# Ten Strassen pairs that accumulate two partial sums in PSUM banks, and a last product in two column halves

## The chip, the cores and the metric

The kernel runs on one core of a Trainium2 chip. The metric is the device time of one execution in microseconds (us). Lower is better. The engines are named as in the profile: PE is TensorE (PEld its weight loads), DVE is VectorE, ACT is ScalarE, POOL is GpSimd and SP is SyncE, which only issues DMAs here. PSUM is the memory into which PE accumulates, in banks of 128x512 fp32; SBUF is the on-chip memory for everything else.

## What the kernel must compute

One block of a hybrid encoder, in fp32, for 1024 positions of width 1024 (cut to what matters):

```python
h = rmsnorm(x, norm_g)
proj = h @ w_in                       # split into q, k, v, za, u, vs, zs, gm
q, k = partial_rope(q), partial_rope(k)
a = window_sink_attention(q, k, v, att_sinks)            # 16 heads, 2 kv heads, window 128
a = (a * silu(za)) @ w_att_out
sgo = chunked_spatial_gating(gelu(u), gelu(vs), sg_w, sg_b, sg_ln_g, sg_ln_b)
sgo = (sgo * silu(zs)) @ w_sg_out
ga, gs = split(sigmoid(gm + b_merge))                    # one merge gate per branch
y = ga * a + gs * sgo
out = rmsnorm(x + y @ w_o, final_g)
```

## The kernel before

**Products.** fp32 accuracy is reached by splitting every operand into a high part in fp32r and a low part that holds the rest (`split`: ACT copies the high part, DVE subtracts it). `product` (L340) multiplies four 128-row blocks of the contraction, three terms each (high x high, high x low, low x high), so it is 12 matmuls of 128x512 into one bank.

**Pairs.** The large products run in the Strassen-Winograd form: `gemm_pair` (L358) handles two 128-row blocks of output as a 2x2 block product with seven products instead of eight. The weights' parts 0 to 6 (w11, w12, the sums s1 to s4 and w22, made on DVE or by DMAs) stand in tiles `wh` and `wl`; the activations' seven forms b11, t1, t2, b21, t3, b22 and t4 stand in the tiles `T_...h` and `T_...l`. The order in a pair is this. b11 goes into the accumulator `acc` (a bank of the pool mm), which ACT copies to x11 (L368). t1 goes into a bank of the pool o, named t5; ACT writes its negative to x22 (L372). t2 accumulates on acc, and ACT copies that to x12 (L375). b21 goes into a fresh bank (pool tp or o), and DVE adds it to x11 (L380): output block (0, 0). t3 accumulates on acc; DVE subtracts acc from x22 (L385): block (1, 1). b22 accumulates on t5; DVE adds it to x12 (L389): block (0, 1). t4 accumulates on acc: block (1, 0). x11, x12, x22 and the tile for block (1, 0) are `xtile()`s, a ring of five SBUF tiles of 128x512. Each is given to the caller's `finish`, which works on it in place and stores it to DRAM; a tile can be taken again when its store has landed.

**Stages.** In order of time: RMSNorm and the forms of its result; the pairs of u, vs and k and v; of q; of z and of the merge gates with attention between their products (`softmax_stage` L1271, whose pieces run as hooks of the pairs); four pairs of za; four s pairs (the spatial branch's output product); four a pairs (attention's output product); the first products of the four token pairs (L1821 to L1825); the token pairs p = 0 to 3 with w_o, the residual, and the last RMSNorm. `finish` of za is Silu on ACT, later a multiply on DVE (`finish_silu`, L1558 and L1559) and a store to a_dr through POOL's queue (`put`, L466). That of an s pair is a Sigmoid gate on ACT (L1684), a multiply on DVE (L1691 or L1693) and a store to y_dr through POOL's queue. That of an a pair is the same with a DMA on POOL's queue that adds onto y_dr; for the last a pair DVE adds what is there (L1788) and SP stores it. The forms t1 to t4 of the next stage are read back from these stores and made between the products: sums by DMAs that add (`bq<-bq`, L202 on POOL's queue), high parts on ACT (L154, L159) and low parts on DVE (L155, L160).

**What sets the order.** The program is written in one order by hand; each engine executes its own instructions strictly in that order, waiting at each for semaphores. `hook` and `split_next` put pieces of other work between the products. `after` adds an order without a wait, and `paced` lets a DMA wait for the last result named in `pace`.

**Attention.** In a step of `softmax_stage` PE makes the scores of two halves c = 0, 1 into banks of the pool sc (L1295), DVE finds the largest by two operations per half (L1303 and L1304, the bound), and ACT takes four exponentials with it (L1308), which release the banks. `split_q` (L1087) splits rotated queries into high parts (ACT, L1092) and low parts (DVE, L1094) and stores both through SP.

**The end.** For the last token pair, p = 3, the order of the products is b22, t3, b21, t4. `add_and_square` (L1846) adds a product to the residual on DVE (L1849) and sums squares on ACT (L1851); `rstd_of` (L132) makes the reciprocal root with a Sqrt on ACT and five small operations on DVE, the last two at L146 and L147; `scale_and_store` (L1861) multiplies by the root and by the gain `g_out`, on ACT (L1868) or DVE (L1871), and stores.

## Time and profile before

| | |
|---|---|
| three runs shown | 1278.79, 904.73 and 905.77 us; median 905.77 |
| the profiled execution, its own time | 905.2 us |
| its span, first to last instruction | 903.4 us |
| around the span | 1.8 us |
| granted clock of PE | 0.998 |
| PE, DVE, ACT and POOL busy | 890.3, 691.3, 529.3 and 149.5 us |
| pairs of za | from 588 to 664 us |
| s pairs, then a pairs | 664 to 741, 742 to 819 us |
| first products of the token pairs, then the token pairs | 819.5 to 830.4, 830.4 to 896 us |

Times in the profile count from the first instruction. A row of the timeline gives the start in us, the duration in us, the engine, the line, the operation, output<-inputs, shapes, and in brackets how long the engine stood idle just before and what released it. Names of tiles stand without their numbers. PE's matmuls follow each other every 0.227 us while a row shows some 0.39 us for one, since they are pipelined and their ends are modelled. A group's row gives after the bar its busy time in us, the mean in ns of one instruction, and the idle time before them with its releasers. In the chain of waits a row names what the end was waiting for at that time.

### The profile page before, as it was taken

The page shows a single profiled execution, that of the slowest core. Times are in us where ns is not written, and L with a number is a line of the kernel's source. Part 1 is how long each engine was busy: PE and PEld are TensorE (multiplying, and loading weights), DVE is VectorE, ACT ScalarE, POOL GpSimd, SP SyncE. Part 2 cuts the span into 40 slices and gives each one's busy share as a digit, 9 for nine tenths or more (in the row PEclk, how much of TensorE's full clock was granted, in tenths as well). Part 3 has the DMA queues.
Part 4 walks back from the last instruction along what each step waited for, and adds up shares of the span by engine and source line. Part 5 has one row for each costly group of instructions (what it writes and reads, how often), then busy time and mean ns, then how long its engine had stood idle before and what let it go on. Part 6 is the DMA issues. An engine that isn't in the chain of part 4 may idle for free.

```text
span 903.4 us, 13232 instructions
## 1 busy us (share of the span) xinstructions
PE 890.3 (99%) x4292; PEld 742.7 (82%) x4292; DVE 691.3 (77%) x1259; ACT 529.3 (59%) x1061; POOL 149.5 (17%) x213
## 2 busy tenths in 40 slices
PE   8999999999999999999999999999999999999996
PEld 6788888888888888888888888888877887888885
DVE  7879966666686788887878888747797488579996
ACT  7865533334445567667677676654675375467443
POOL 2322222203030001111110111101121121110012
PEclk9999999999999999999999999999999999999999
DMA  9998888958778768888687789899899788998632
GB/s 328 212 246 227 264 204 176 171 152 266 255 251 284 216 181 215 209 168 207 177 230 224 232 247 234 209 332 352 301 291 339 287 230 241 301 301 263 208 120 113
DMA packets 132750, 213.77 MB, mean 237 GB/s; under 512 B 12777, under 2 KB 61161, under 8 KB 132682
## 3 DMA queue, kind: packets, MB, share of 16 engines
q1 hardware_dynamic: 110072, 149.74, 50.0%
q0 software_dynamic: 22464, 62.93, 31.3%
q8 instruction: 34, 0.56, 0.3%
q14 instruction: 34, 0.28, 0.1%
q10 hardware_dynamic: 146, 0.27, 0.1%
HBM read 147.74 MB, written 86.11 MB: 259 GB/s over the span
## 4 chain that ended last, share of the span: by engine, by line
PE 82%; DMA 8%; issue 7%; ACT 1%; POOL 1%; DVE 1%; SPq 0%; POOLq 0%; ACTq 0%; DVEq 0%
PE ps_mm L350 34%; PE ps_o L350 26%; PE ps_sc L1295 3%; PE ps_tp L708 2%; PE ps_sc L350 2%; PE ps_mm L708 2%; PE ps_o L1380 2%; PE ps_o L708 2%; PE ps_tp L1339 2%; DMA bq<-bq 2%; PE ps_tp L970 2%; PE ps_tp L350 2%; DMA a_dr<-x 1%; PE ps_sc L708 1%; DMA y_dr<-x 1%
## 5 line engine op out<-in xcount | busy, mean ns | idle before, releaser
L159 ACT CAST wh<-s 128x1024 fp32r<-128x1024 f32 (+1 forms) x79 | 79.2, 1005 | 89.3 <-PE ps_mm L350 42.7
L160 DVE TENSOR_TENSOR wl<-wr,wh 128x512 fp32r<-128x512 f32 (+1 forms) x77 | 72.1, 937 | 51.3 <-ACT wh L159 50.4
L160 DVE TENSOR_TENSOR wl<-s,wh 128x1024 fp32r<-128x1024 f32 (+1 forms) x79 | 92.6, 1173 | 11.6 <-ACT wh L159 11.5
L159 ACT CAST wh<-wr 128x512 fp32r<-128x512 f32 (+1 forms) x77 | 63.1, 820 | 59.9 <-PE ps_mm L350 33.4
L350 PE MATMUL ps_o<-T_t1h,wh 128*128 128x512 f32 x148 | 58.6, 396 | 0.0
L350 PE MATMUL ps_o<-T_b22h,wh 128*128 128x512 f32 x148 | 58.3, 394 | 0.0
L350 PE MATMUL ps_o<-T_t1h,wl 128*128 128x512 f32 x148 | 57.8, 391 | 0.0
L350 PE MATMUL ps_o<-T_b22l,wh 128*128 128x512 f32 x148 | 57.8, 391 | 0.0
L350 PE MATMUL ps_o<-T_b22h,wl 128*128 128x512 f32 x148 | 57.7, 390 | 0.0
L350 PE MATMUL ps_o<-T_t1l,wh 128*128 128x512 f32 x148 | 57.6, 389 | 0.0
L350 PE MATMUL ps_mm<-T_t3h,wh 128*128 128x512 f32 x140 | 55.1, 394 | 1.5 <-ACT x L375 1.5
L1308 ACT ACTIVATE pr<-ps_sc,sm 128x192 f32<-128x192 f32 (+2 forms) x128 | 50.8, 409 | 8.8 <-DVE sm L1304 6.3
L350 PE MATMUL ps_mm<-T_t4h,wh 128*128 128x512 f32 x140 | 55.1, 394 | 0.2 <-DVE x L385 0.2
L350 PE MATMUL ps_mm<-T_b11h,wh 128*128 128x512 f32 x140 | 54.9, 392 | 0.0
L350 PE MATMUL ps_mm<-T_b11h,wl 128*128 128x512 f32 x140 | 54.7, 391 | 0.0
L350 PE MATMUL ps_mm<-T_t4h,wl 128*128 128x512 f32 x140 | 54.7, 391 | 0.0
L350 PE MATMUL ps_mm<-T_b11l,wh 128*128 128x512 f32 x140 | 54.7, 391 | 0.0
L350 PE MATMUL ps_mm<-T_t3h,wl 128*128 128x512 f32 x140 | 54.7, 391 | 0.0
L350 PE MATMUL ps_mm<-T_t2h,wl 128*128 128x512 f32 x140 | 54.6, 390 | 0.0
L350 PE MATMUL ps_mm<-T_t2h,wh 128*128 128x512 f32 x140 | 54.6, 390 | 0.0
L350 PE MATMUL ps_mm<-T_t2l,wh 128*128 128x512 f32 x140 | 54.5, 390 | 0.0
L350 PE MATMUL ps_mm<-T_t4l,wh 128*128 128x512 f32 x140 | 54.5, 389 | 0.0
(400 smaller groups left out, 2396.7 us busy)
## 6 DMA issues: line engine op xcount, KB each, us to landing
wr<-in_w_dram SPq DMA_DIRECT2D x86, 256.0 KB
sums<-in_w_dram POOLq DMA_DIRECT2D x20, 512.0 KB, 6.8
s<-sums SPq DMA_DIRECT2D x20, 512.0 KB
q_hl<-qhl SPq DMA_DIRECT2D x16, 512.0 KB
q<-q_hl SPq DMA_DIRECT2D x64, 128.0 KB
y_dr<-x POOLq DMA_DIRECT2D x28, 256.0 KB, 6.9
g<-in_w_dram POOLq DMA_DIRECT2D x12, 512.0 KB, 6.6
wr<-in_w_dram SPq DMA_DIRECT2D x11, 512.0 KB
```

The source lines that it names most:

```text
L159: hi_of.append(nc.scalar.copy(hi, src))
L160: return nc.vector.tensor_sub(lo, src, hi.bitcast(F32))
L350: nc.tensor.matmul(acc, lt, rt, start=fresh and k == 0 and n == 0, stop=k == 3 and n == 2, skip_group_check=True,)
L708: mm = nc.tensor.matmul(acc[:], lt, rt, start=fresh and k == 0 and n == 0, stop=k == 3 and n == terms[-1], skip_group_check=True,)
L970: nc.tensor.matmul(pm[:, t * P : (t + 1) * P], xh[:, half * 4 + t, g * P : (g + 1) * P], bias[-1][1][:, g % 4, :], start=True, stop=True,)
L1295: nc.tensor.matmul(sc[:, i, k0:], q_of[:, c, i * P : (i + 1) * P], kt[:, f, k0:], start=f == 0, stop=f == 1,)
L1308: nc.scalar.activation(held_in[c, i], sc[:, i, lo:hi], AF.Exp, bias=nmax[:, c, i : i + 1], scale=-1.0, accum_out=sums[:, c, i : i + 1],)
L1339: nc.tensor.transpose(dst, pr[:, i, block * P : block * P + width], ident[:])
L1380: nc.tensor.matmul(po[:, cs], lt, rt, start=n == 0, stop=n == len(terms) - 1)
```

## The change

1. `gemm_pair_in_banks` (new) takes the place of `gemm_pair` in ten pairs: the last two of za, all four of s and all four of a. x11 and x12 are there two banks of the pool tp, to which ACT copies acc, from PSUM to PSUM. PE accumulates b21 onto x11 and b22 onto x12, so DVE's addition of L380 is gone and `finish` reads block (0, 0) from its bank. The negative of t1 is an x tile, `minus5`, which stays until both differences are made: block (1, 1) is minus5 - acc and block (0, 1) is x12 - minus5, each in an x tile of its own. A pair takes five x tiles instead of four.
2. In attention's first step DVE takes the two low parts of q (L1094) that stood ahead of the bounds one behind each bound.
3. The last product of the last token pair, t4, is made in two column halves: 24 matmuls of 128x256 into two banks of the pool sc. What had been accumulated before is added to the residual earlier; each half has its own addition and sum of squares. `rstd_of` has a variant that leaves out one small operation of DVE and gives -2 times the root; the gain of that row, `g_last`, is -0.5 times `g_out`, which ACT makes in p = 2. ACT's multiply of the first row's half is ordered behind the last Sqrt.

```diff
+    def gemm_pair_in_banks(b, finish, hook):
...
+        acc, x11, x12 = bank("mm")[:], bank("tp")[:], bank("tp")[:]
+        product(acc, ready[n, 0], b["b11"], True)
+        pace[0] = nc.scalar.copy(x11, acc)
+        hook()
+        t5 = bank("o")[:]
+        product(t5, ready[n, 2], b["t1"], True)
+        minus5 = xtile()
+        pace[0] = nc.scalar.mul(minus5[:], t5, -1.0)
+        hook()
+        product(acc, ready[n, 3], b["t2"], False)
+        pace[0] = nc.scalar.copy(x12, acc)
+        split_next()
+        hook()
+        product(x11, ready[n, 1], b["b21"], False)
+        finish(0, 0, xtile(), x11, 1.0)
+        split_next()
+        hook()
+        product(acc, ready[n, 4], b["t3"], False)
+        q = xtile()
+        term[0] = nc.vector.tensor_sub(q[:], minus5[:], acc)
+        finish(1, 1, q, q[:], 1.0)
+        hook()
+        product(x12, ready[n, 5], b["b22"], False)
+        q = xtile()
+        term[0] = nc.vector.tensor_sub(q[:], x12, minus5[:])
+        finish(0, 1, q, q[:], 1.0)
+        split_next()
+        hook()
+        product(acc, ready[n, 6], b["t4"], False)
+        finish(1, 0, xtile(), acc, -1.0)
...
-            nc.vector.tensor_tensor(nmax[:, c, :], nmax[:, c, :], nsk, op=ALU.min)
+            bound = nc.vector.tensor_tensor(nmax[:, c, :], nmax[:, c, :], nsk, op=ALU.min)
+            if n_pr[0] == 1:
+                after(lows_of_q[c - 2], bound)
...
-        gemm_pair(sb_, finish, part_of_loads if m else last_form(s_forms, part_of_loads), "tp")
+        gemm_pair_in_banks(sb_, finish, part_of_loads if m else last_form(s_forms, part_of_loads))
...
-        product(acc, ready[n, 6], ob["t4"], False)
-        add_and_square(1, 0, acc, 1.0)
+        z = xr[:, 2, :]
+        nc.vector.tensor_add(z, z, acc)
+        wide = HALF // 2
+        for e in range(2):
+            cs = slice(e * wide, (e + 1) * wide)
+            part = bank("sc")[:, 0:wide]
+            h, l = ob["t4"]
+            product(part, ready[n, 6], (h[:, :, cs], l[:, :, cs]), True)
+            pace[0] = nc.vector.tensor_add(z[:, cs], z[:, cs], part)
+            ss = mtile([P, 1], F32, "st1", 16)
+            nc.scalar.activation(bank("tp")[:, 0:wide], z[:, cs], AF.Square, accum_out=ss[:])
...
```

The change also moves instructions, which the diff doesn't show. Below are rows of the compiled programs: line, operation, output<-inputs with the tiles' numbers, shape, and the semaphores waited for (DMASW and DMAHW are DMA queues of POOL and SP, the rest engines). The changed kernel has more lines, so its numbers are higher.

ScalarE in the first s pair, before; x_6940, x_6942 and x_6941 are x11, x22 and x12, and ps_mm is acc:

```order
L368 COPY x_6940<-ps_mm_6939 128x512 [waits DMASW1_49,PE_49]
L372 ACTIVATE x_6942<-ps_o_6956 128x512 [waits DMASW5_49,PE_49]
L159 COPY T_t3h_6927<-bq_1138_6296 128x1024 [waits DVE_49] x2
L159 COPY wh_6983<-wr_6727 128x512 [waits DMAHW1_49,PE_49,Activation_49]
L375 COPY x_6941<-ps_mm_6939 128x512 [waits DMASW7_49,PE_49]
L159 COPY T_t4h_6987<-bq_1188_6589 128x1024 [waits DMASW4_49]
L159 COPY T_t4h_6987<-bq_1188_6589 128x1024 [waits DMASW6_49]
L1684 ACT_TABLE_LOAD [waits DMAHW6_49,DMAHW5_49]
```

The same place after; ps_tp_6942 and ps_tp_6943 are the new x11 and x12, and x_6970 is minus5:

```order
L409 COPY ps_tp_6942<-ps_mm_6941 128x512 [waits PE_49,Activation_49]
L414 ACTIVATE x_6970<-ps_o_6957 128x512 [waits PE_49]
L162 COPY T_t3h_6929<-bq_1138_6296 128x1024 [waits DVE_49] x2
L162 COPY wh_6985<-wr_6728 128x512 [waits DMAHW1_49,PE_49,Activation_49]
L417 COPY ps_tp_6943<-ps_mm_6941 128x512 [waits PE_49]
L162 COPY T_t4h_6989<-bq_1188_6589 128x1024 [waits DMASW4_49]
L162 COPY T_t4h_6989<-bq_1188_6589 128x1024 [waits DMASW6_49]
```

The order is the same, but none of the three copies waits for a DMA any more. VectorE at the same place, before:

```order
L160 TENSOR_TENSOR T_t4l_6988<-bq_1188_6589,T_t4h_6987 128x1024 [waits DMASW4_49,Activation_49]
L160 TENSOR_TENSOR T_t4l_6988<-bq_1188_6589,T_t4h_6987 128x1024 [waits DMASW6_49,Activation_49]
L380 TENSOR_TENSOR x_6940<-x_6940,ps_tp_6993 128x512 [waits DMASW1_49,PE_49]
L160 TENSOR_TENSOR wl_7013<-wr_6877,wh_7012 128x1024 [waits DMAHW4_49,Activation_49]
L1693 TENSOR_TENSOR x_6940<-x_6940,g_1238_6889 128x512 [waits DVE_49]
L385 TENSOR_TENSOR x_6942<-x_6942,ps_mm_6939 128x512 [waits DMASW5_49,PE_49]
L389 TENSOR_TENSOR x_6941<-x_6941,ps_o_6956 128x512 [waits DMASW7_49,PE_49]
L1693 TENSOR_TENSOR x_6942<-x_6942,g_1239_6891 128x512 [waits DVE_49,Activation_49]
L1693 TENSOR_TENSOR x_6941<-x_6941,g_1240_6893 128x512 [waits DVE_49,Activation_49]
```

And after, where x_7007, x_7029 and x_7048 are the tiles of blocks (0, 0), (1, 1) and (0, 1), and L1744 is the gate's multiply:

```order
L163 TENSOR_TENSOR T_t4l_6990<-bq_1188_6589,T_t4h_6989 128x1024 [waits DMASW4_49,Activation_49]
L163 TENSOR_TENSOR T_t4l_6990<-bq_1188_6589,T_t4h_6989 128x1024 [waits DMASW6_49,Activation_49]
L1744 TENSOR_TENSOR x_7007<-ps_tp_6942,g_1242_6891 128x512 [waits DMASW5_49,PE_49,Activation_49]
L163 TENSOR_TENSOR wl_7014<-wr_6879,wh_7013 128x1024 [waits DMAHW4_49,Activation_49]
L426 TENSOR_TENSOR x_7029<-x_6970,ps_mm_6941 128x512 [waits DMASW7_49,PE_49]
L431 TENSOR_TENSOR x_7048<-ps_tp_6943,x_6970 128x512 [waits DMASW0_49,PE_49]
L1744 TENSOR_TENSOR x_7029<-x_7029,g_1243_6893 128x512 [waits DVE_49,Activation_49]
L1744 TENSOR_TENSOR x_7048<-x_7048,g_1244_6895 128x512 [waits DVE_49,Activation_49]
```

The addition of b21 is gone, the multiply that waits for the gate stands ahead of the low part wl instead of behind it, and the DMA waits (DMASW5, DMASW7, and a new one, DMASW0) are now on the multiply and the two differences. On PE the b11 matmuls of the next pair that stand ahead of t4 become three of twelve instead of five in the first s pair, and two instead of five in the first a pair.

ScalarE between the a pairs and the token pairs, before; g_1484 and g_1486 are copies of first products, T_t4h is the high part of w_o's form t4, and wh_8171 and wh_8175 are weights' parts of the first token pair:

```order
L159 COPY T_b22h_8213<-bq_1477_8210 128x1024 [waits DMAHW4_49,PE_49]
L159 COPY T_b22h_8213<-bq_1477_8210 128x1024 [waits DMAHW7_49]
L1823 COPY g_1484_8229<-ps_sc_8228 128x512 [waits DVE_49,PE_49]
L1823 COPY g_1486_8244<-ps_sc_8243 128x512 [waits DVE_49,PE_49,Activation_49]
L159 COPY T_t4h_8222<-bq_1480_8219 128x1024 [waits DMAHW7_49]
L159 COPY wh_8171<-s_8165 128x1024 [waits DVE_49]
L159 COPY wh_8175<-wr_8156 128x512 [waits DMAHW2_49,Activation_49]
L159 COPY wh_8175<-s_8166 128x512
L159 COPY T_t4h_8222<-bq_1480_8219 128x1024 [waits DMAHW1_49]
```

And after:

```order
L162 COPY T_b22h_8223<-bq_1497_8220 128x1024 [waits DMAHW4_49,PE_49]
L162 COPY T_b22h_8223<-bq_1497_8220 128x1024 [waits DMAHW2_49]
L162 COPY T_t4h_8232<-bq_1500_8229 128x1024 [waits DMAHW3_49,PE_49]
L162 COPY T_t4h_8232<-bq_1500_8229 128x1024 [waits DMAHW4_49]
L1874 COPY g_1504_8239<-ps_sc_8238 128x512 [waits DVE_49,PE_49]
L1874 COPY g_1506_8254<-ps_sc_8253 128x512 [waits DVE_49,PE_49,Activation_49]
L162 COPY wh_8181<-s_8175 128x1024 [waits DVE_49]
L162 COPY wh_8185<-wr_8166 128x512 [waits DMAHW1_49,Activation_49]
L162 COPY wh_8185<-s_8176 128x512
```

Both casts for t4 now stand ahead of the two copies, and no cast for t4 stands ahead of or between wh_8181 and wh_8185; SP issues the load of their source earlier.

More of the change, by code (lines that the diff above doesn't have):

```diff
@@ L1853, in add_and_square @@
                 scaled[i, half] = mtile([P, HALF], F32, gtag(), 1, pool)
-                nc.gpsimd.tensor_tensor(scaled[i, half][:], z, g_out[:, half, :], op=ALU.mult)
+                gain = (g_last if i else g_out)[:, half, :]
+                nc.gpsimd.tensor_tensor(scaled[i, half][:], z, gain, op=ALU.mult)
             if i in sq:
@@ L1867, in scale_and_store @@
                     v = scaled[i, e][:]
-                    nc.scalar.mul(v, v, r[:])
+                    by_root = nc.scalar.mul(v, v, r[:])
+                    if i == 0:
+                        after(by_root, of_root[-1])
                     (nc.scalar if i else nc.sync).dma_start(out[row, half_of(e)], v)
                     continue
-                by_gain = nc.vector.scalar_tensor_tensor(z, z, r[:], g_out[:, e, :], op0=ALU.mult, op1=ALU.mult)
+                gain = (g_last if p == 3 and i else g_out)[:, e, :]
+                by_gain = nc.vector.scalar_tensor_tensor(z, z, r[:], gain, op0=ALU.mult, op1=ALU.mult)
                 if p < 3 or i == 0:
@@ L1880, in hybrid_tile @@
         product(acc, ready[n, 3], ob["t2"], False)
-        nc.scalar.copy(x12[:], acc)
+        copied = nc.scalar.copy(x12[:], acc)
+        if p == 2:
+            after(nc.scalar.mul(g_last, g_out, -0.5), copied)
         if p:
@@ L1923, in hybrid_tile @@
         by_b21()
[L1924 to L1925 removed]
+        z = xr[:, 2, :]
[9 more added lines that the diff above has]
+            nc.scalar.activation(bank("tp")[:, 0:wide], z[:, cs], AF.Square, accum_out=ss[:])
+            if e == 0:
+                base = mtile([P, 1], F32, "st1", 16)
+                nc.vector.scalar_tensor_tensor(base[:], ss[:], 1.0 / D, sq[1][:], op0=ALU.mult, op1=ALU.add)
+            else:
+                sq[1] = rstd_of(ss[:], 1.0 / D, base[:], times_minus_2=True)
         scale_and_store(0)
```

26 lines of the change are left out of this document (20 added, 6 removed).

## The prediction, made before the changed kernel was run

> **What bounds the kernel now.** I read the page first: its table of engines.
>
> ```profile
> PE 890.3 (99%) x4292; PEld 742.7 (82%) x4292; DVE 691.3 (77%) x1259; ACT 529.3 (59%) x1061; POOL 149.5 (17%) x213
> ```
>
> TensorE works 890.3 of 903.4 us, and the change removes no matmul. So it can win only TensorE's idle time and the ends: 13 us in all, under 2% of the time (18.1 us), which is about what a measurement of this kernel can tell from no change. What there is to win must stand in single stalls, so I read the waits of TensorE next, and then laid the first t1 matmuls of neighbouring pairs against each other. A pair is 84 matmuls, and the distance between two such rows is a pair's time.
>
> ```profile
> PE ps_mm L350 <- ACT x L375: 1.5, 2, 1.0
> 590.86 0.39 PE L350 MATMUL ps_o<-T_t1h,wh 128*128 128x512 f32 x1
> 609.89 0.39 PE L350 MATMUL ps_o<-T_t1h,wh 128*128 128x512 f32 x1
> 667.01 0.39 PE L350 MATMUL ps_o<-T_t1h,wh 128*128 128x512 f32 x1
> 688.15 0.39 PE L350 MATMUL ps_o<-T_t1h,wh 128*128 128x512 f32 x1
> 745.27 0.39 PE L350 MATMUL ps_o<-T_t1h,wh 128*128 128x512 f32 x1
> 765.08 0.39 PE L350 MATMUL ps_o<-T_t1h,wh 128*128 128x512 f32 x1
> ```
>
> An undisturbed pair takes 609.89 - 590.86 = 19.03 us: 0.227 per matmul, 2.72 per product. The first s pair takes 21.14, so it loses 2.11; the first a pair takes 19.81 and loses 0.78. The view of waits shows only 1.5 of this, since it counts idle time from modelled ends. The rows of the stalls and of what ScalarE waited for, with two pieces of the chain of waits:
>
> ```profile
> 676.37 0.50 PE L350 MATMUL ps_mm<-T_t3h,wh 128*128 128x512 f32 x1 [1.03 <-ACT x L375]
> 683.70 0.50 PE L350 MATMUL ps_mm<-T_t4h,wh 128*128 128x512 f32 x1 [0.22 <-DVE x L385]
> 754.07 0.50 PE L350 MATMUL ps_mm<-T_t3h,wh 128*128 128x512 f32 x1 [0.48 <-ACT x L375]
> 664.07 11.58 DMA a_dr<-x
> 670.65 0.60 ACT L372 ACTIVATE x<-ps_o 128x512 f32<-128x512 f32 x1 [1.78 <-DMA a_dr<-x]
> 675.73 0.58 ACT L375 COPY x<-ps_mm 128x512 f32<-128x512 f32 x1 [2.08 <-DMA a_dr<-x]
> 743.19 10.16 DMA y_dr<-x
> 753.43 0.58 ACT L375 COPY x<-ps_mm 128x512 f32<-128x512 f32 x1 [2.08 <-PE ps_tp L350]
> ```
>
> ScalarE's copy of x12 must empty the accumulator before t3 may add to it, but its target is an x tile of a ring of five, still being stored. The store of 664.07 lands at 675.65 and the copy starts at 675.73; that of 743.19 lands at 753.35 and the copy starts at 753.43. The releaser named in the last row, a product, ended earlier.
>
> **The change part by part.** *Ten pairs.* x11 and x12 now go to PSUM banks, which wait for no store; b21 and b22 accumulate there. The store waits move to VectorE: to the first multiply of a pair, to the difference minus5 - acc and to x12 - minus5. In the first s pair, undisturbed, t3 starts at 667.01 + 3 x 2.72 = 675.17 and ends at 677.89; only then is the difference possible, and its store has landed at 675.65: 2.2 us of cover. The multiply's store (that of 670.65) is covered by the end of b21 at 675.17. In the first a pair minus5, on ScalarE, still waits for the store that x22 waits for now:
>
> ```profile
> 748.19 0.60 ACT L372 ACTIVATE x<-ps_o 128x512 f32<-128x512 f32 x1 [1.69 <-PE ps_o L350]
> ```
>
> x22 ran as soon as t1 was done, so that store had landed by 748.19, and the copy behind minus5 isn't due before t2 ends at 745.27 + 5.44 = 750.71.
>
> What is late next? The casts and lows for t4:
>
> ```profile
> 676.21 2.00 ACT L159 CAST T_t4h<-bq 128x1024 fp32r<-128x1024 f32 x2
> 678.23 1.28 ACT L1684 ACT_TABLE_LOAD   x1
> 681.22 1.23 DVE L160 TENSOR_TENSOR wl<-wr,wh 128x1024 fp32r<-128x1024 f32 x1 [0.97 <-ACT wh L159]
> 682.97 0.68 DVE L385 TENSOR_TENSOR x<-x,ps_mm 128x512 f32<-128x512 f32 x1
> ```
>
> I lay these durations out in the new order. minus5 starts when t1 ends, at 669.73; with it (0.60), t3's two casts (2.00 like t4's), a small cast and the copy (about 0.6 each), x12 is copied by 673.6 and t4's casts end at 675.6. From the table load's start to wl's start is 681.22 - 678.23 = 2.99 today, with the sigmoid and a cast between; that puts wl at 678.6 to 679.8 and the difference at 680.5. (VectorE's first multiply now stands ahead of wl; it waits for that sigmoid and lies within the 2.99.) t4 is due when b22 ends, at 680.61, plus the b11 matmuls now ahead of it (three of 0.227): 681.3. The margin is 0.8. So I book the whole 2.11: the stall at t3 and that at t4 both stand behind one copy. In the first a pair t4 waits for nothing even now, and ScalarE moves ahead with TensorE: 0.78 booked.
>
> *New copies.* ScalarE has never copied from bank to bank here. Nearest rows:
>
> ```profile
> L1851 ACT ACTIVATE ps_tp<-bq 128x512 f32<-128x512 f32 x16 | 9.6, 600 | 22.8 <-DVE bq L1849 22.8
> L978 DVE SCALAR_TENSOR_TENSOR ps_tp<-ps_tp,lg_sb,bias 128x512 f32<-128x512 f32 x16 | 11.9, 752 | 0.0
> ```
>
> So the price is between 0.58 (the copy into SBUF at 675.73) and 0.75 (VectorE from bank to bank); I take 0.60, the row of the same engine that writes a bank. The bank is read two products (5.4 us) after the copy can start, and the longest thing ahead of it on ScalarE is a pair of casts (2.00), so either end is hidden: nothing. Ten additions (x11 + t2) leave VectorE, and the sign of one difference changes; both lie beside a TensorE that doesn't wait for them: nothing. If that cover went, an addition would bring or cost what a copy does.
>
> *Bridge to the last stage.* Here t4's casts now stand ahead of the copies of the first products.
>
> ```profile
> 827.65 1.05 ACT L159 CAST T_t4h<-bq 128x1024 fp32r<-128x1024 f32 x1 [1.89 <-DMA bq<-g]
> 829.67 1.23 DVE L160 TENSOR_TENSOR wl<-s,wh 128x1024 fp32r<-128x1024 f32 x1 [1.50 <-ACT wh L159]
> 830.36 0.39 PE L350 MATMUL ps_o<-T_t1h,wh 128*128 128x512 f32 x1
> 830.96 0.50 PE L350 MATMUL ps_o<-T_t1h,wl 128*128 128x512 f32 x1
> 833.36 0.39 PE L350 MATMUL ps_sc<-T_t2h,wh 128*128 128x512 f32 x1
> ```
>
> t1 of the first token pair takes 833.36 - 830.36 = 3.00 instead of 2.72, since its third matmul wants a low part that is finished at 830.90: ScalarE stood before t4's cast for 1.89 us. With the load issued earlier this goes: 0.28 at most, nothing at least; I take 0.28, since 1.89 us ahead of the low part is far more than it is late.
>
> *Attention's first step.* The two lows of q go behind the bounds, so ScalarE's exponentials begin and release their banks earlier.
>
> ```profile
> 306.82 1.05 PE L1295 MATMUL ps_sc<-k,q 128*128 128x128 f32 x8
> 310.52 1.32 PE L1295 MATMUL ps_sc<-k,q 128*128 128x128 f32 x8
> 312.07 2.99 SPq L1242 DMA_DIRECT2D q<-q_hl  x4
> 317.69 1.11 PE L1295 MATMUL ps_sc<-k,q 128*128 128x256 f32 x8
> ```
>
> The second step's scores take 1.32 against 1.05: 0.27 lost, and booked. The delayed lows hold up q's stores and the q loads on SP's queue by, as I estimate, 1 us; those loads serve the scores at 317.69, some 4 us after the first two are issued. Bounds: 0.27 gained, about 1 lost if that cover fails.
>
> *The end.* The last t4 product becomes two column halves.
>
> ```profile
> 568.91 1.11 PE L1295 MATMUL ps_sc<-k,q 128*128 128x256 f32 x8
> 568.91 0.91 PEld L1295 LDWEIGHTS ps_sc<-k,q 128*128 128x128 f32 x7
> 569.86 0.40 PE L1380 MATMUL ps_o<-pT,v 128*128 128x256 f32 x2
> 896.13 0.69 DVE L1849 TENSOR_TENSOR bq<-bq,ps_mm 128x512 f32<-128x512 f32 x1
> 898.58 0.16 DVE L147 TENSOR_TENSOR st<-st,st 128x1 f32<-128x1 f32 x1
> 898.77 0.72 ACT L1868 ACTIVATE g<-g,st 128x512 f32<-128x512 f32 x1 [0.87 <-DVE st L147]
> ```
>
> Eight 128x256 matmuls take 569.86 - 568.91 = 0.95, so 24 take 2.86 against 2.72: 0.14 lost. The half addition and half Square save, by estimate, 0.27 and 0.17 of 0.69 and 0.60. One small operation of VectorE less saves 898.77 - 898.58 = 0.19. VectorE's queue has the chain of row 0 and the base of the first half ahead of the last addition; I estimate that it starts 0.2 late for that. Net 0.27 + 0.17 + 0.19 - 0.14 - 0.2 = 0.3 gained; bounds: nothing, if the queue is twice as late and more, and 0.5, if it isn't late.
>
> A rule of the Trainium skill speaks against halving. TensorE: Matmul & The Clock Gate, section "The mechanism" (packing small matmuls), says that weight loads overlap running matmuls only when the row group differs. All matmuls here use all rows, so by that rule each half pays its load as well, as in the worse case of the third rival. The trace disagrees: seven loads lie inside the 0.95 us of eight matmuls.
>
> *Sum.* 2.11 + 0.78 + 0.28 + 0.27 + 0.30 = 3.74; I keep back 0.15 for waits too small to see. The profiled execution took 905.2 us (span 903.4 and 1.8 around it), so 905.2 - 3.6 = 901.6 us. The median of the three runs shown, 905.77, is 0.6 above it.
>
> **The rivals.** *The wait only moves* (0.14): the store waits now on VectorE, or minus5, hold t3, t4 or the lows as long as before. For it: stores that take 10 to 12 us, and a strict order on VectorE, where the multiply that waits for the sigmoid now stands ahead of wl. Against: margins of 0.9 and 2.2 us. Only attention and the end remain: 905.2 - 0.57 = 904.6.
>
> *Given back later* (0.08): the last stage has VectorE nearly full.
>
> ```profile
> 831.00:893.00 62.00, 62.00 (x274) 51.30 (x275) 56.62 (x113) 28.95 (x63) 7.28 (x13) 1.00 0.46 158
> ```
>
> Its columns after the first are the busy times of PE, PEld, DVE, ACT and POOL: VectorE 56.6 of 62 us. If its work or its loads don't move ahead with TensorE, half the gain is lost: 903.4. Against: TensorE is dense there today.
>
> *Halves paced by their weight loads* (0.06), which a 128x512 matmul hides and a half may not:
>
> ```profile
> L350 PEld LDWEIGHTS ps_mm<-T_t4h,wh 128*128 128x128 f32 x140 | 26.3, 188 | 5.6 <-DVE x L385 0.7
> ```
>
> 24 loads of 0.188 take 4.5 us, 1.65 more than 2.86: 903.3. If loads and matmuls didn't overlap at all, 24 x (0.188 + 0.119) = 7.4 would give 906.1 (0.01 of the 0.06). Against both: the rows at 568.91, and 0.227 per matmul today, where 0.188 + 0.227 would show.
>
> *Slower* (0.08): products b21 and b22, which used to start a fresh bank, now wait for ScalarE's copies. It decides once a copy comes later than its cover. The ten pairs give back 3.6 at 0.36 each; at 0.5 each the time is 906.6. Against: the copy would have to end over 5 us after its product, and ScalarE is 59% busy.
>
> **How the numbers follow.** The forecast has 0.64, the rivals 0.14, 0.08, 0.06 and 0.08. The range reaches from 900.7 (every term at its upper bound, nothing kept back, and 0.5 for the spread between 904.73 and 905.2) to 904.8, which takes in all but the slower rival and the worse case of the third; the chance left out is about 0.1, and as much again for terms that I have not thought of. Faster by over 2% would need 887 us, less than TensorE's own work: 0.01. Slower by over 2% is in no case: 0.01. Within 2%: 0.98.
>
> **What would show it.** First t1 rows of the first s and a pairs 19.0 to 19.1 us from the next; no wait of TensorE on an x copy; the first token pair's t1 at 2.72; the second scores near 1.05; 24 halves in 2.9 us and the last multiply about 0.3 nearer to the last product's start. I am wrong if VectorE's differences show a wait on a store that TensorE follows, if t4 in the first s pair waits, if b21 or b22 wait for ScalarE, or if the scores at 317.69 come late.

## The result, and the profile after

The changed kernel takes 901.31 us (median of 6 runs, 900.38 to 902.31) beside 904.94 for the kernel before (median of 6 runs); the ratio is 0.9957, with a 95% interval from 0.9945 to 0.9969. That is within 2%, and clear of noise: 3.6 us less in the medians. The forecast was 901.6. The profiled execution took 901.17 us, with a span of 899.4, 4.0 under the 903.4 of before. One run of the kernel before took 1278.79 us: the median of 904.94 counts it (904.73 without it), the ratio leaves it out.

The distances between the first t1 matmuls of neighbouring pairs say where the 4.0 us come from. The last column is the prediction's term.

| place | before | after | difference | predicted |
|---|---|---|---|---|
| first t1 of all (untouched code) | 99.20 | 98.80 | -0.40 | none |
| from there to attention's first pair (untouched code) | 208.50 | 208.67 | +0.17 | none |
| attention's first pair | 24.21 | 23.94 | -0.27 | -0.27 |
| first s pair | 21.14 | 19.19 | -1.95 | -2.11 |
| first a pair | 19.81 | 19.04 | -0.77 | -0.78 |
| first token pair | 16.60 | 16.32 | -0.28 | -0.28 |
| last product's first matmul to ScalarE's last store | 6.31 | 5.79 | -0.52 | -0.30 |

The first two rows are the same instructions in both kernels; over the fourteen profiles of this study the first of them lies between 98.24 and 99.20. They are a part of the difference between two executions, not of the change.

The page's table of engines after: on TensorE 12 matmuls of 128x512 have become 24 of half the width, VectorE works 5.5 us less and ScalarE 2.7 us more.

```profile
PE 889.1 (99%) x4304; PEld 743.7 (83%) x4304; DVE 685.8 (76%) x1251; ACT 532.0 (59%) x1064; POOL 149.8 (17%) x213
```

All of TensorE's waits after (line waited for, us in total, times, longest). No wait on an x copy or a difference is left in this view; the three belong to the first 100 us, which the change doesn't touch.

```profile
PE ps_sc L555 <- DVE T_b22l L544: 2.2, 1, 2.2
PE ps_mm L750 <- ACT T_b11h L647: 0.7, 1, 0.7
PE ps_sc L634 <- DVE wr L629: 0.4, 1, 0.4
```

The timeline of TensorE: first t1 matmuls of the first and second s pair, the first and second a pair and the first token pair, and the first t2 matmul of that pair. Their distances are 19.19, 19.04 and 2.72.

```profile
666.56 0.39 PE L353 MATMUL ps_o<-T_t1h,wh 128*128 128x512 f32 x1
685.75 0.39 PE L353 MATMUL ps_o<-T_t1h,wh 128*128 128x512 f32 x1
742.87 0.39 PE L353 MATMUL ps_o<-T_t1h,wh 128*128 128x512 f32 x1
761.91 0.39 PE L353 MATMUL ps_o<-T_t1h,wh 128*128 128x512 f32 x1
827.19 0.39 PE L353 MATMUL ps_o<-T_t1h,wh 128*128 128x512 f32 x1
829.91 0.39 PE L353 MATMUL ps_sc<-T_t2h,wh 128*128 128x512 f32 x1
```

The first s pair after, from the timelines of ScalarE, VectorE and TensorE. ScalarE's copy of x12 starts 5.99 us behind the pair's first t1 matmul instead of 8.72, so 2.7 us earlier, and waits for nothing. VectorE then works without a gap from 676.10 to the difference (L426), which ends at 680.79, while t4 is due at 680.84, 63 matmuls of 0.227 us behind the first t1. The 0.15 us that this pair still loses stand there: the next matmul comes 0.34 us later instead of 0.23.

```profile
672.55 0.58 ACT L417 COPY ps_tp<-ps_mm 128x512 f32<-128x512 f32 x1
676.10 2.35 DVE L163 TENSOR_TENSOR T_t4l<-bq,T_t4h 128x1024 fp32r<-128x1024 f32 x2
678.37 0.68 DVE L1744 TENSOR_TENSOR x<-ps_tp,g 128x512 f32<-128x512 f32 x1
678.97 1.21 DVE L163 TENSOR_TENSOR wl<-wr,wh 128x1024 fp32r<-128x1024 f32 x1
680.11 0.68 DVE L426 TENSOR_TENSOR x<-x,ps_mm 128x512 f32<-128x512 f32 x1
680.84 0.49 PE L353 MATMUL ps_mm<-T_t4h,wh 128*128 128x512 f32 x1
681.18 0.39 PE L353 MATMUL ps_mm<-T_t4l,wh 128*128 128x512 f32 x1
```

The end after: first and one of the last half matmuls, the second half's addition, its Square, the last root, and ScalarE's store. The addition starts 0.3 us after the matmul at 892.50 started, as soon as the product is there; VectorE isn't late for it.

```profile
889.75 0.28 PE L353 MATMUL ps_sc<-T_t4h,wh 128*128 128x256 f32 x1
892.50 0.28 PE L353 MATMUL ps_sc<-T_t4h,wl 128*128 128x256 f32 x1
892.82 0.42 DVE L1990 TENSOR_TENSOR bq<-bq,ps_sc 128x256 f32<-128x256 f32 x1
893.27 0.39 ACT L1992 ACTIVATE ps_tp<-bq 128x256 f32<-128x256 f32 x1 [0.92 <-DVE bq L1990]
893.81 0.29 ACT L137 ACTIVATE st<-st,st 128x1 f32<-128x1 f32 x1
895.54 0.40 ACTq L1924 DMA_DIRECT2D out_dram<-g  x1
```

### The profile page after: what moved, and what is told of

Same layout as the page of the kernel before. It is cut to its first block, busy times and chain, and to the rows that moved or that the text cites. A ratio compares the mean times of both kernels' runs of the same rounds, so it can differ in the third digit from the quotient of the medians.

```text
span 899.4 us, 13233 instructions
## 1 busy us (share of the span) xinstructions
PE 889.1 (99%) x4304; PEld 743.7 (83%) x4304; DVE 685.8 (76%) x1251; ACT 532.0 (59%) x1064; POOL 149.8 (17%) x213
## 4 chain that ended last, share of the span: by engine, by line
PE 97%; DMA 1%; ACT 1%; DVE 0%; issue 0%; SPq 0%
PE ps_mm L353 42%; PE ps_o L353 27%; PE ps_tp L353 7%; PE ps_sc L1341 3%; PE ps_sc L353 3%; PE ps_tp L750 2%; PE ps_o L1428 2%; PE ps_tp L1387 2%; PE ps_mm L750 2%; PE ps_o L750 2%; PE ps_tp L1012 2%; PE ps_sc L750 1%; PE ps_sc L634 1%; DMA T_t3h<-in_w_dram 1%; ACT wh L162 0%
## 5 line engine op out<-in xcount | busy, mean ns | idle before, releaser
L353 PE MATMUL ps_mm<-T_t3l,wh 128*128 128x512 f32 x140 | 54.5, 389 | 0.0
L307 POOL DMA_DIRECT2D sums<-in_w_dram x40 | 29.8, 939 | 91.6 <-ACT x L371 42.2
L353 PE MATMUL ps_o<-T_b22h,wh 128*128 128x512 f32 x108 | 42.7, 395 | 0.0
```

The costliest lines, as they stand in the source:

```text
L307: return lambda: paced(nc.gpsimd.dma_start(dst, src, accum_op=op))
L353: nc.tensor.matmul(acc, lt, rt, start=fresh and k == 0 and n == 0, stop=k == 3 and n == 2, skip_group_check=True,)
```

## The experiments

The theory: the gain in the pairs is a store wait taken off the accumulator. Only the first s and the first a pair had one; the eight other pairs gain nothing in themselves. The rival: accumulating in the banks, with VectorE's additions gone, is what pays. Each run was timed beside the kernel before on its own chip, whose median was 905.5 to 906.1 there, 0.6 to 1.1 above the first comparison; so differences and ratios are compared, not times across jobs. The profiles give the places (all in us):

| run | attention's first pair | first s | first a | first token | end |
|---|---|---|---|---|---|
| before | 24.21 | 21.14 | 19.81 | 16.60 | 6.31 |
| after | 23.94 | 19.19 | 19.04 | 16.32 | 5.79 |
| banks_only | 24.16 | 19.26 | 19.05 | 16.32 | 6.31 |
| ends_only | 24.22 | 21.75 | 20.36 | 16.45 | 5.79 |
| two_pairs | 24.19 | 19.71 | 19.07 | 16.38 | 5.79 |
| held_x12 | 24.16 | 19.46 | 19.04 | 16.47 | 6.30 |
| copies_plus2 | 24.24 | 19.55 | 19.04 | 16.32 | 5.78 |
| copies_plus4 | 24.26 | 27.73 | 21.94 | 16.40 | 5.79 |
| quarters | 23.95 | 19.10 | 19.09 | 16.32 | 8.60 |
| whole_last | 23.95 | 19.09 | 19.04 | 16.32 | 6.12 |
| late_gate | 23.94 | 19.24 | 19.06 | 16.32 | 5.80 |
| three_pairs | 24.17 | 19.90 | 19.07 | 16.32 | 5.79 |
| five_pairs | 23.95 | 19.60 | 19.07 | 16.31 | 5.80 |
| early_q | 23.95 | 19.63 | 19.05 | 16.32 | 5.80 |

### The banks alone

```diff
 the kernel before, with
+    def gemm_pair_in_banks(b, finish, hook):
 and its ten calls; attention and the end as before
```

> The ten pairs with banks, without the edits to attention and to the end. Theory (the pairs' gain is a store wait taken off the accumulator, and the edits add up): first s pair 19.2 us and first a pair 19.04 from one first t1 matmul to the next, t1 of the first token pair 2.72, the second scores still 1.3, the end as before; about 3.0 us under the kernel before, 902.0. Rival (fewer VectorE additions pay in every pair): undisturbed pairs under 19.03.

902.11 us (median of 11) beside 905.5; ratio 0.9954 (0.9932 to 0.9976), 3.4 less. First s pair 19.26, first a pair 19.05, first token pair 16.32 with t1 at 2.72, the end 6.31 as before; no pair of za, s or a under 19.03. As the theory has it; the places sum to 3.0.

### Attention and the end alone

```diff
 the changed kernel, with
-            gemm_pair_in_banks(hb, finish, lambda: part_of_s(m))
+            gemm_pair(hb, finish, lambda: part_of_s(m), "tp")
 and the same for s and a
```

> The edits to attention and to the end, no pair with banks. Theory (the edits add up): second scores 1.05, the end 0.5 us shorter, first s and a pairs still 21.1 and 19.8, t1 of the first token pair still 3.0; 0.8 us under the kernel before, 904.1. Rival (the edits need each other, since the last stage only gains where it is entered earlier): no gain at the end.

905.53 us (median of 11) beside 905.5; ratio 0.9993 (0.9970 to 1.0016). The 0.8 us that were expected are inside the interval, and so is nothing. The places tell more. The second scores take 1.05 and the end is 5.79, both as expected, so the end gains without the banks. But attention's pair still takes 24.22, and the two store waits on ScalarE are longer in this profile than before, 2.87 instead of 2.08 in the first s pair and 2.63 instead of 2.08 in the first a pair, though neither the code nor the order differs there. ScalarE in the first s pair of this run, and its piece of the chain of waits:

```profile
664.58 11.60 DMA a_dr<-x
676.26 0.58 ACT L378 COPY x<-ps_mm 128x512 f32<-128x512 f32 x1 [2.87 <-DMA a_dr<-x]
```

The store took 11.60 us here and 11.58 before; it was issued 0.5 us later. So the old stall has no fixed size: it is what remains of a store's flight, and 2.1 and 2.7 us of it were seen in one pair.

### Banks in two pairs only

```diff
 the changed kernel, with
+        if m:
+            gemm_pair(sb_, finish, part_of_loads, "tp")
+        else:
+            gemm_pair_in_banks(sb_, finish, last_form(s_forms, part_of_loads))
 the same for a, and gemm_pair for za
```

> Banks in the first s and the first a pair alone; attention and the end as changed. Theory (eight of the ten pairs gain nothing in themselves): 19.2 and 19.04, but t1 of the first token pair back at 3.0, since the order at that place is moved by the last a pair; 3.5 us under the kernel before, 901.4. Rival (all ten pairs are needed, since the ring of tiles is used otherwise): one of the two pairs still waits, 902.5 or more.

901.4 us (median of 12) beside 905.5; ratio 0.9959 (0.9950 to 0.9968). Two of ten pairs bring what ten bring, within the interval. The first a pair took 19.07; the first s pair 19.71, more than the 19.2 expected, and t1 of the first token pair 2.78, less than 3.0 but over 2.72: the order there is the old one, and ScalarE's first cast for t4 waits 1.67 us in it (1.89 before). What the first s pair lost shows on ScalarE, the second cast for t4:

```profile
674.67 1.05 ACT L162 CAST T_t4h<-bq 128x1024 fp32r<-128x1024 f32 x1 [1.07 <-DMA bq<-bq]
```

Not a store, as the rival had it, but the DMA that sums t4's source is late here. From this cast hang the table load, the gate, wl and the difference, and t4 waited 0.33 us for that. Whether the za pairs have to do with it was left to a later run.

### x12 held in a bank, every addition as before

```diff
 the kernel before; in the first s and the first a pair
-        x11, x12, x22 = xtile(), xtile(), xtile()
+        x11, x12, x22 = xtile(), bank("sc"), xtile()
...
-        term[0] = nc.vector.tensor_add(x12[:], x12[:], t5)
-        finish(0, 1, x12, x12[:], 1.0)
+        q = xtile()
+        nc.scalar.copy(q[:], x12[:])
+        term[0] = nc.vector.tensor_add(q[:], q[:], t5)
+        finish(0, 1, q, q[:], 1.0)
```

> The kernel before, but in the first s and the first a pair x12 is copied into a free bank, and from there into an x tile when b22 is done; every addition is still VectorE's. Theory (the store wait ahead of t3 is the cause): 19.2 to 19.5 and 19.04 in the two pairs, 2.4 us under the kernel before, 902.5. Rival (accumulating in the bank, so fewer additions on VectorE, is what pays): 21.1 and 19.8, 904.9.

902.7 us (median of 12) beside 905.5; ratio 0.9964 (0.9942 to 0.9986), 2.8 less. 19.46 and 19.04, as the theory expected. Nothing is accumulated in these banks and no addition is saved, and ScalarE has one copy more in each of the two pairs, so the rival is out: what pays is that the copy which empties the accumulator has a target that no store holds. ScalarE in the first s pair: the write of x22 still waits for its store, the copy of x12 behind it for nothing.

```profile
670.67 0.60 ACT L411 ACTIVATE x<-ps_o 128x512 f32<-128x512 f32 x1 [1.99 <-DMA a_dr<-x]
673.57 0.59 ACT L414 COPY ps_sc<-ps_mm 128x512 f32<-128x512 f32 x1
```

### Each bank copy made three times

```diff
+        for _ in range(2):
+            nc.scalar.copy(x11, acc)
         pace[0] = nc.scalar.copy(x11, acc)
 and the same ahead of the copy to x12
```

> The changed kernel with each copy into a bank made three times, so it ends some 1.1 us later. Theory (the copy is covered up to the next product on the accumulator, one product or 2.72 us after it can start): nothing lost where ScalarE is free, at most a few tenths of a us where casts stand ahead; 901.3 to 902.5. The prediction's cover of 5.4 us: nothing lost at all. The slower rival: each of the ten pairs loses, 906 or more.

906.41 us (median of 10) beside 905.57; ratio 1.0014 (1.0005 to 1.0024). The gain is gone and 0.8 us with it: the time is the slower rival's, against both counts of cover, but it isn't lost as the rival had it, in each pair. TensorE's waits:

```profile
PE ps_mm L353 <- ACT ps_tp L411: 2.8, 4, 0.9
PE ps_mm L353 <- ACT ps_tp L421: 1.2, 1, 1.2
```

Five stalls, at t2 four times and at t3 once: in the last za, the first s, the last s and (twice) the last a pair. The other pairs of za, s and a take 19.04 as ever. Four of the five stalls don't show what a delay of 1.1 us costs, since the edit did more there: in the last za, s and a pairs casts of the next stage's high parts came to stand between the copies. ScalarE in the last za pair, first the one copy of the changed kernel, then this run:

```profile
647.78 0.57 ACT L409 COPY ps_tp<-ps_mm 128x512 f32<-128x512 f32 x1 [0.78 <-PE ps_mm L353]
```

```profile
648.64 1.05 ACT L162 CAST T_b11h<-bq 128x1024 fp32r<-128x1024 f32 x1
649.59 0.59 ACT L410 COPY ps_tp<-ps_mm 128x512 f32<-128x512 f32 x1
650.11 1.04 ACT L162 CAST T_b11h<-bq 128x1024 fp32r<-128x1024 f32 x1
651.05 0.59 ACT L411 COPY ps_tp<-ps_mm 128x512 f32<-128x512 f32 x1
```

Counted from the pair's first t1 matmul, the last copy ends at 3.7 us instead of 0.8, and t2 is due at 2.7. Only in the first s pair does the edit do little more than it says: the copy ends at 3.0 instead of 2.2, and t2 waits 0.20 us. So the cover was there: in the changed kernel the copies to x11 end 1.9 us ahead of t2 in the last za, s and a pairs, 1.3 us in the first a pair and 0.5 us in the first s pair, where two casts stand ahead. And the wait is at t2 and t3 on the accumulator, not at b21 and b22, which is where the prediction's slower rival had put it.

### Each bank copy made five times

```diff
-        for _ in range(2):
+        for _ in range(4):
```

> Each copy into a bank made five times, so it ends some 2.1 us later, 2.9 us after its product at the earliest. Theory of one product's cover: t2 and t3 wait for ScalarE in most of the ten pairs, 0.2 us or more each, 4 to 12 us lost in all. The prediction's cover of 5.4 us: nothing lost in the products, at most some tenths from later casts.

945.1 us (median of 4) beside 905.57; ratio 1.0445 (1.0427 to 1.0464). Now the pairs between lose too: 21.02 instead of 19.04. ScalarE and TensorE in such a pair; t1 began at 703.05 and needs 2.72, so t2 is due at 705.77, and it starts when the fifth copy is done.

```profile
703.25 2.38 ACT L410 COPY ps_tp<-ps_mm 128x512 f32<-128x512 f32 x4 [1.21 <-PE ps_mm L353]
705.65 0.57 ACT L411 COPY ps_tp<-ps_mm 128x512 f32<-128x512 f32 x1
706.28 0.50 PE L353 MATMUL ps_mm<-T_t2h,wh 128*128 128x512 f32 x1 [0.35 <-ACT ps_tp L411]
```

This settles the cover: it is one product (2.72 us) from the moment the copy can start, since t2 goes onto the accumulator that the copy reads. The prediction's 5.4 us, up to the product that reads the bank, were never available. The loss is larger than the 4 to 12 us expected, 40 us, since casts stand between the copies in this run too, later casts are delayed (wh, 9.0 and 2.1 us of waits), and the long stalls lowered the clock (last section).

### The last product in quarters

```diff
-        wide = HALF // 2
+        wide = HALF // 4
-        for e in range(2):
+        for e in range(4):
```

> The changed kernel with the last product in four column parts, 48 matmuls of 128x128. Theory (a narrow matmul is paced by its own weight load, as the 0.11 us of attention's 128x128 scores say): 48 x 0.11 = 5.3 us instead of 2.9, the last addition and Square shorter by 0.3; 2.1 us above the changed kernel. Rival 1 (paced by columns): 2.9 us, 0.2 us under the changed kernel. Rival 2 (loads don't overlap with matmuls at all): 48 x (0.188 + 0.06) = 11.9 us, 9 us above.

904.0 us (median of 10) beside 905.57; ratio 0.9985 (0.9973 to 0.9996), 2.2 us above whole_last (the next run), which was timed with it. The end takes 8.60 instead of 5.79. Weight loads and matmuls of TensorE in it:

```profile
889.44 0.19 PEld L353 LDWEIGHTS ps_sc<-T_t4l,wh 128*128 128x128 f32 x1
889.55 0.19 PEld L353 LDWEIGHTS ps_sc<-T_t4h,wl 128*128 128x128 f32 x1
```

```profile
889.49 0.28 PE L353 MATMUL ps_sc<-T_t4l,wh 128*128 128x128 f32 x1
889.61 0.27 PE L353 MATMUL ps_sc<-T_t4h,wl 128*128 128x128 f32 x1
```

A matmul of 128 columns goes every 0.11 us, as one load does, though a half of 256 columns goes every 0.12: under 256 columns narrower pieces win nothing more here. Beside that, a third quarter must wait 0.3 us for a bank that VectorE still reads. That the loads overlap with matmuls and with each other (0.19 long, 0.11 apart) is sure from these rows; whether the load or something else in the matmul sets the 0.11 isn't told apart.

### The last product whole

```diff
-        wide = HALF // 2
+        wide = HALF
-        for e in range(2):
+        for e in range(1):
```

> The changed kernel with the last product whole: 12 matmuls of 128x512 into one bank, one addition, one Square. Theory (0.16 lost on the product's longer way, 0.28 and 0.21 saved on addition and Square): the end, from the first matmul of the last product to ScalarE's store, 6.1 us instead of 5.8, 0.3 us above the changed kernel. Rival (the halves gain nothing, the shorter chain of small operations is all): no difference.

901.75 us (median of 5) beside 905.57; ratio 0.9961 (0.9948 to 0.9974). The end takes 6.12, against 5.79 in halves and 6.31 before. So of the 0.52 gained there, the halves bring 0.33 and the shorter chain behind them 0.19. The total can't tell 0.3; the trace can.

### The first multiply behind the first difference

```diff
 in the first s pair
-        finish(0, 0, xtile(), x11, 1.0)
         split_next()
         hook()
         product(acc, ready[n, 4], b["t3"], False)
+        first = xtile()
         q = xtile()
         term[0] = nc.vector.tensor_sub(q[:], minus5[:], acc)
+        finish(0, 0, first, x11, 1.0)
```

> The changed kernel, but in the first s pair the multiply of block (0, 0), with its gate on ScalarE, comes behind the first difference. Theory (what is left of that pair's loss, 0.15 us, is VectorE's backlog ahead of the difference): 19.04 in the first s pair, no stall at t4; 0.15 us under the changed kernel, which the total can hardly show. Rival (the rest has another cause, the new wait of the difference on its store among them): 19.2 as before, or more.

900.95 us (median of 6) beside 905.84; ratio 0.9942 (0.9929 to 0.9956). The first s pair takes 19.24, not 19.04. The difference and the matmuls of t4:

```profile
679.12 0.67 DVE L428 TENSOR_TENSOR x<-x,ps_mm 128x512 f32<-128x512 f32 x1
```

```profile
679.63 0.39 PE L353 MATMUL ps_tp<-T_b22h,wl 128*128 128x512 f32 x1
679.94 0.47 PE L353 MATMUL ps_mm<-T_t4h,wh 128*128 128x512 f32 x1
680.25 0.39 PE L353 MATMUL ps_mm<-T_t4l,wh 128*128 128x512 f32 x1
```

Counted from the pair's first t1 the difference ends 0.7 us earlier than in the changed kernel, so VectorE's backlog was real. But the compiled order gave that away: t4 follows b22 at once here, where three b11 matmuls of the next pair (0.68 us) stood between. The difference ends 0.07 us before t4 is due here and 0.05 before in the changed kernel, so the run moved t4's date along with it and can't settle the expectation.

Three other profiles tell more. In quarters and whole_last the first s pair is the changed kernel's; the difference ended 0.13 us before t4 was due, and the pair lost 0.06 and 0.05. In banks_only it ended 0.03 after, and the pair lost 0.22. So the loss follows the end of the difference, and thereby VectorE's queue; what made that late is told with five_pairs, below.

### Banks in three pairs, and in five

```diff
 the changed kernel; banks only where
+        if m == 0:                # s
+        if m in (0, 6):           # a
 (three_pairs), and in the last two za pairs as well (five_pairs)
```

> Banks in the first s, the first a and the last a pair alone; attention and the end as changed. Theory (the bridge's gain is the order moved by the last a pair, the seven others gain nothing): 19.2, 19.04 and 2.72, as fast as the changed kernel, 901.3. Rival (the bridge gains from the loads of earlier pairs): t1 of the first token pair still over 2.9.

> Banks in the last two za pairs, the first s, the first a and the last a pair; attention and the end as changed. The first s pair took 19.7 and 19.9 us where the za pairs had no banks, since the second cast for t4 waited over 1 us for a DMA that sums its source, and 19.1 to 19.3 where they had. Theory (the za pairs' change is what lets that sum land earlier): no such wait, 19.1 to 19.3. Rival (the sum's landing varies from run to run, whatever the za pairs do): a wait of about 1 us, 19.6 or more. Time in the first case that of the changed kernel, 901.3, in the second 0.6 more.

three_pairs: 901.99 us (median of 5) beside 905.84; ratio 0.9953 (0.9939 to 0.9967). The first token pair takes 16.32 with t1 at 2.72: the last a pair is the one that moves the order there. In the first s pair, 19.90, the second cast for t4 waited 1.30 us for the same DMA as in two_pairs.

five_pairs: 901.25 us (median of 6) beside 906.06; ratio 0.9954 (0.9941 to 0.9968). The first s pair took 19.60, and ScalarE waited again at t4's second cast although the za pairs had their banks:

```profile
676.44 1.05 ACT L162 CAST T_t4h<-bq 128x1024 fp32r<-128x1024 f32 x1 [0.93 <-DMA bq<-bq]
```

The second s pair, without banks in this run, took 19.40; ScalarE waited 1.20 us there for a load of gates, and no run shows whether banks would have covered that. For the wait the rival is right: that sum lands early or late from run to run, whatever the za pairs do. early_q, with the ten pairs of the change, waited 0.48 us for it and took 19.63.

But the wait at t4's cast is not what cost these two runs most. From 0.3 us into the pair up to the difference VectorE has no gap in early_q, and one of 0.04 us in five_pairs: it entered the pair late, since ScalarE's second cast for t2, ahead of the pair, had waited for another DMA of sums. That row in early_q:

```profile
664.06 1.06 ACT L157 ACTIVATE T_t2h<-bq 128x1024 fp32r<-128x1024 f32 x1 [0.69 <-DMA bq<-bq]
```

In the profiles with banks in the za pairs the pair's loss goes with this wait: none in whole_last and quarters (0.05 and 0.06 lost), 0.22 us in the changed kernel (0.15), 0.30 in banks_only (0.22), 0.52 in five_pairs (0.56) and 0.69 in early_q (0.59). In two_pairs and three_pairs t2's cast waited for nothing, and there t4's cast did hold up VectorE, by 0.24 us in the one and by 0.33 and 0.25 us in the other. What sets the landing of either sum wasn't found.

### Queries loaded earlier

```diff
 in attention's first step
+                if n == 0:
+                    for store in stores_of_q[-4:]:
+                        after(store, loads_of_q[-1])
```

> The changed kernel, with the queries of attention's third step loaded ahead of the last four stores of q instead of behind them on SyncE. Theory (where the third scores start 0.15 us late and take 1.03 instead of 0.95, they wait for these loads, whose landing is the next thing behind the bounds): the loads are issued some 3 us earlier, the third scores wait for nothing, that pair takes 23.94 us. Rival (another wait): 24.2 as in six of the ten runs. Time 0 to 0.25 us under the changed kernel, which the total can hardly show.

901.26 us (median of 6) beside 906.06; ratio 0.9948 (0.9934 to 0.9962). The question came from ends_only and two_pairs: the second scores were at 1.05 there, and still the pair took 24.2. TensorE in ends_only at the third scores; the matmul before started at 317.04, so they start 0.15 late:

```profile
317.04 0.39 PE L353 MATMUL ps_o<-T_b21h,wl 128*128 128x512 f32 x1
317.42 1.20 PE L1341 MATMUL ps_sc<-k,q 128*128 128x256 f32 x8
```

This happened in five of the ten other profiles that have the change to attention (five, not the six of the expectation), and not in the five others, after among them. In early_q the loads are issued at 308.61, 1.4 us into the pair instead of 4.4, and the third scores wait for nothing:

```profile
308.61 1.89 SPq L1291 DMA_DIRECT2D q<-q_hl  x2
```

```profile
316.71 0.39 PE L353 MATMUL ps_o<-T_b21h,wl 128*128 128x512 f32 x1
316.94 1.11 PE L1345 MATMUL ps_sc<-k,q 128*128 128x256 f32 x8
```

That fits the theory, but one profile can't show it, since five others had no wait either; the trace names no releaser where there was one. As a version, it is as fast as the changed kernel, not measurably faster.

## Why the prediction was right, and where its steps were not

- **The bound.** Right: nothing but single stalls and the end was to be had, and the 4.0 us of span came from the places named, beside 0.2 of untouched code.
- **The store wait at t3** (2.11 and 0.78 booked, 1.95 and 0.77 measured). The cause is shown: held_x12 takes this wait away, with every addition kept, and brings 2.8 us, and two_pairs brings the same as ten. The size was that of one profile; in ends_only, with the same code in these pairs, they lost 2.71 and 1.32.
- **The margin of 0.8 at the first s pair's t4** (0.9 where the rivals are weighed). Wrong, though only 0.15 us hung on it in this profile: 0.05 was left. ScalarE's chain came as worked out, its table load 8.6 us behind the pair's first t1 matmul. The working left out VectorE's own queue, which was full from 670.96 on: t4's lows started at 676.10, when ScalarE's casts had been done for a us, so wl began 0.8 and the difference ended 0.7 us later than worked out. How late that queue is hangs on when DMAs of sums land, and the working had no term for it: in four later profiles one came later still (t4's in two_pairs and three_pairs, t2's in five_pairs and early_q), and this pair lost 0.6 to 0.9. That the booked 2.11 came so near is in part luck of this one profile.
- **The new copies.** Price right (0.57 and 0.58 in the changed kernel, 0.60 taken), cover wrong: one product, not two. "Nothing" held all the same, since every copy ends at least 0.5 us ahead of the product that waits for it.
- **The bridge** (0.28 booked and measured). The cause was right, the order of ScalarE's casts; three_pairs shows that the last a pair moves it. The size was again that of one profile: with the old order t1 lost 0.28 before, but 0.13, 0.06 and 0.15 in ends_only, two_pairs and held_x12. With the new order it takes 2.72 in nine of ten profiles (2.80 in copies_plus4).
- **Attention** (0.27 booked and measured). The second scores gain it. But in five of the eleven profiles with this part of the change the third scores start late and the pair takes 24.17 to 24.26, so that the whole 0.27 shows in this profile is luck too. The prediction named q's loads as the bound there and estimated that they would be held up by 1 us; they are issued 4.4 us behind the pair's first t1 matmul, before and after. Whether they are what the third scores wait for isn't shown.
- **The end** (0.30 booked, 0.52 measured). The mis-sized term is the 0.2 for VectorE's queue: the second addition starts right behind its product. The rest was right: the product's way 0.16 longer (0.14), addition 0.28 shorter (0.27), Square 0.21 (0.17), the small operation 0.19.
- **The rivals.** The wait did not move: the differences wait for no store. (The 904.6 of that rival left out the bridge, which doesn't hang on a store.) Nothing was given back in the last stage, whose token pairs take 16.32 as before. Halves go every 0.12 us, not every 0.188. The slower case begins with copies 0.5 us later than they are in the first s pair, and elsewhere with more.

## What to carry to other kernels

When a stall stands behind a copy, ask what the copy's target is still waiting for before asking how to make the copy cheaper: another target of the same price removed the stall here with every addition kept. Cover is counted up to the next instruction that needs the buffer the operation releases, here the accumulator, not up to the one that reads its result. One profile gives one size of a wait on a DMA: margins of under a us were used up here by other executions of the same code. And an edit that is meant to delay one operation can also change what stands ahead of it; the order in the trace has to be read before the time is.

## What the runs showed of the hardware that was not expected

In copies_plus4 the stalls were long enough to lower TensorE's clock. The window of the first such stall and the two after it (columns: window, its length, busy us and instructions of PE, PEld, DVE, ACT and POOL, granted clock, DMA share, GB/s):

```profile
652.20:655.90 3.70, 0.38 (x2) 0.00 (x0) 2.24 (x3) 3.70 (x7) 0.00 (x0) 1.00 1.03 398
655.90:659.40 3.50, 3.45 (x8) 2.78 (x9) 3.19 (x4) 0.96 (x1) 1.76 (x2) 0.52 0.83 259
659.40:662.00 2.60, 2.60 (x13) 2.07 (x12) 0.69 (x1) 1.61 (x3) 0.00 (x0) 0.99 1.01 189
```

TensorE stood still for 3.4 us, and for the next 3.5 us it was granted 0.52 of its clock: 8 matmuls where 15 fit, 1.6 us lost after the stall had ended. This happened five times in the run, with stalls of 3.4, 4.1, 3.3, 3.3 and 2.1 us. By the granted clock in windows of 0.2 us it fell at 656.0, 683.3, 751.6, 840.3 and 850.6, each time to 0.50 and for 3.4 us. The distances are 8, 20, 26 and 3 times 3.413 us, so the clock falls on a fixed beat and not when a stall ends: the second fall came 1.0 us after its stall had ended at 682.32, the fourth 0.5 us before its own had. The beat ahead of the last fall, that fall and the beat after it:

```profile
847.17:850.58 3.41, 1.28 (x6) 0.78 (x5) 2.95 (x3) 3.41 (x6) 0.00 (x0) 1.00 0.55 165
850.58:853.99 3.41, 3.41 (x9) 2.50 (x8) 3.14 (x4) 3.41 (x6) 0.00 (x0) 0.50 0.75 250
853.99:857.40 3.41, 3.41 (x16) 2.80 (x15) 0.93 (x3) 2.25 (x3) 0.00 (x0) 1.00 0.56 212
```

2.1 us of standing still in a beat of 3.4 were enough there; 1.7 us in the beat from 676.49 to 679.90 were not, and the stalls of 1 to 1.7 us between matmuls elsewhere in this study lowered nothing. The Trainium skill, TensorE: Matmul & The Clock Gate, section "Part 1: The HAM clock gate", says that the clock is halved after an idle window of about 3.4 us and comes back after a busy one of the same length, and that the window runs freely. These rows agree in the half, the length and the free run; that a window needn't be idle throughout is what the last fall adds.
